# A hybrid encoder layer on one core: VectorE and ScalarE in written order within the attention stage

## The chip, the cores and the metric

The kernel runs on one core of a Trainium2 chip. A core has TensorE (matmuls, PE in the rows; PEld are its weight loads), VectorE (DVE), ScalarE (ACT), GpSimd (POOL) and SyncE (SP, which issues most DMAs). The metric is the time of one execution on the device in microseconds; lower is better. The kernel before takes 2234.18 us, the median of three runs (2233.41 to 2234.49).

## The reference

One layer of an encoder for 2048 tokens of width 1024: a modulated RMS norm, one input projection, windowed attention (8 query heads and 2 key heads of 64) beside a bidirectional mLSTM (4 heads of 128), a norm for each, one output projection, and a SwiGLU network. The attention and the place of the mLSTM's output gate `o_m` are what the change touches:

```python
proj = hmix @ w_in
q_a, k_a, v_a, q_m, k_m, v_m, o_m, gates = jnp.split(proj, IN_SPLITS, axis=-1)
att = banded_attention(q_a, k_a, v_a, sink)      # |t-s| <= 128, blocks of 128
att = rms_norm(att, g_attn_out)
...
h_m = rms_norm(h_fwd + h_bwd, g_mlstm_out)
h_m = jax.nn.sigmoid(o_m) * h_m
mix = jnp.concatenate([att, h_m], axis=-1) @ w_out
x = x + gate1 * mix

def banded_attention(q, k, v, sink):
    logits = q @ k.T * hd ** -0.5 - slope * dist     # three key blocks of 128
    mx = jnp.maximum(jnp.max(logits), sink)
    p = jnp.exp(logits - mx)
    p = p / (jnp.sum(p) + jnp.exp(sink - mx))
    return p @ v
```

## The kernel before

A float32 product is made of two or three matmuls on reduced-precision halves: a high half (ScalarE copies and rounds) and a low half (VectorE or GpSimd subtracts).

**The attention stage** is one loop over 32 units and two more steps (`for s_ in range(len(order) + 2)`). A unit is a block of 128 queries for one key head, that is four query heads. Three units are in work at a time. Of the newest, `u0`, each step makes the scores of four heads (`score`: two matmuls into `as` on L928 and L929, VectorE's maximum L932, ScalarE's exponential L934), then the reciprocal of the sum (`adn`) and, on GpSimd, the normalized scores `ap` (L948). Of the one before, `u1`, it makes three transposes (`transpose`: four TensorE instructions into `atp`, L955), each split by `split` into a high half `apth` (ScalarE) and a low half `aptl` (VectorE), both recorded on L140 and L141. Of the oldest, `u2`, it makes the product with the values (`values`: two matmuls for each of three blocks into `ao`, L967 with the high half, L968 with the low), which ScalarE and VectorE bring to `at`.

**Between these**, `pull(n)` puts in n matmuls of a projection that is due (`proj_mm`, tile `gps`, L640, three for each of eight slices of the weights: two with the high half `whi`, one with the low half `wlo`). What is due stands in `fill`: first the query columns of the last two attention heads (`second`, 96 matmuls), then the output-gate columns `o_tiles` of head 1 (96), then those of heads 2 and 3 together, in four parts (`lasts`, 48 each). `pull` also counts the beats after which a delayed action of `put_soon` is issued.

**The weights of a projection** come by `cols_steps`: SP loads 512 KB into `wraw`, a tile with one buffer; ScalarE makes `whi` (L235, 128x1024), GpSimd makes `wlo` in four pieces (L238, 128x256 each). `proj_cols` runs all of it at once. `o_tiles` calls `proj_cols` for all its heads when its first matmul is asked for, so in the program's text the conversions stand where that matmul stands.

**Order.** TensorE's order is the written one in the whole stage (a manual schedule). For VectorE, ScalarE, GpSimd and SP a scheduler orders the instructions; it may issue one ahead of where it is written. `finish_wo`, behind the loop, splits the output weights `wo` (four pairs of tiles of 128x1024); `first_pair` prepares the first tiles of the output projection between steps, and `Pair` holds the two pairs of token tiles with their squares (`msq`), sums (`aps`) and gates.

## Time and profile before

| what | value |
|---|---|
| median of three runs | 2234.18 us (2233.41 to 2234.49) |
| profiled execution | 2234.74 us, its span 2232.6 us |
| TensorE busy | 2211.5 us, 99% of the span |
| TensorE weight loads | 1864.0 us, 83% |
| VectorE | 1586.1 us, 71% |
| ScalarE | 1063.0 us, 48% |
| GpSimd | 1026.6 us, 46% |
| chain that ended last | 92% of it TensorE |

TensorE's matmuls are pipelined, and their ends are modelled: one starts every 0.23 us or so, though each is shown with 0.39. A wait of TensorE is therefore read from the distance of two starts, or from the idle time that a row names, and whether a wait of another engine costs time is read from whether TensorE has work meanwhile.

### The profile page before, as it was taken

What the parts mean: (1) busy time and instruction counts of PE and PEld (TensorE: products, weight loads), DVE (VectorE), ACT (ScalarE), POOL (GpSimd) and SP (SyncE); (2) the same over time, 40 slices, a digit from 0 to 9 for tenths busy, and PEclk for the clock granted to TensorE, in tenths of its full rate; (3) what the DMA queues carried; (4) which work ended last, traced back from release to release, by engine and by line L of the source; (5) the groups of instructions that cost most, each with busy time, mean ns of one, the idle gap of its engine ahead of it and who ended that gap; (6) DMA issues with size and microseconds to landing.
All of it is one profiled execution on the core that took longest, in us unless ns stands there. A gap on an engine that the chain in (4) does not pass through costs nothing.

```text
span 2232.6 us, 32512 instructions
## 1 busy us (share of the span) xinstructions
PE 2211.5 (99%) x10912; PEld 1864.0 (83%) x10912; DVE 1586.1 (71%) x2923; ACT 1063.0 (48%) x2215; POOL 1026.6 (46%) x901
## 2 busy tenths in 40 slices
PE   8999999999999999999999999999999999999998
PEld 8998888888888888888888888888888888888886
DVE  6866768656788898877766777776666665665794
ACT  6524665543778765354544435433433333333452
POOL 0018434444344344446666664566665663591020
PEclk9999999999999999999999999999999999999999
DMA  9468655776766667763353546334233374334552
GB/s 350 159 218 256 203 159 163 213 221 174 213 200 196 200 223 249 256 204 128 105 175 109 177 159 207 123 128 136 91 114 99 113 261 135 129 120 152 196 203 92
DMA packets 337063, 391.28 MB, mean 175 GB/s; under 512 B 20874, under 2 KB 234234, under 8 KB 336896
## 3 DMA queue, kind: packets, MB, share of 16 engines
q1 hardware_dynamic: 335216, 388.39, 53.7%
q8 instruction: 86, 1.41, 0.3%
q10 hardware_dynamic: 1680, 0.82, 0.1%
q14 instruction: 81, 0.66, 0.1%
HBM read 269.95 MB, written 119.19 MB: 174 GB/s over the span
## 4 chain that ended last, share of the span: by engine, by line
PE 92%; ACT 3%; DVE 3%; DMA 1%; issue 1%; SPq 0%; POOL 0%; ACTq 0%; DVEq 0%; POOLq 0%
PE gps L640 15%; PE fp L56 13%; PE fp L58 13%; PE fp L57 13%; PE fo L57 6%; PE fo L56 6%; PE fo L58 6%; PE ops L56 2%; PE ops L58 2%; PE ops L57 2%; PE num L856 1%; PE kvp L769 1%; ACT ap L934 1%; PE num L858 1%; PE pv L56 1%; PE pv L57 1%
## 5 line engine op out<-in xcount | busy, mean ns | idle before, releaser
L640 PE MATMUL gps<-hT,whi 128*128 128x512 f32 x1088 | 396.2, 418 | 0.0
L57 PE MATMUL fo<-w,ah 128*128 128x512 f32 x616 | 239.9, 390 | 0.0
L56 PE MATMUL fo<-w,ah 128*128 128x512 f32 x616 | 239.9, 389 | 0.0
L58 PE MATMUL fo<-w,al 128*128 128x512 f32 x616 | 239.8, 389 | 0.0
L640 PE MATMUL gps<-hT,wlo 128*128 128x512 f32 x544 | 226.5, 416 | 0.0
L640 PEld LDWEIGHTS gps<-hT,whi 128*128 128x128 f32 x1088 | 199.6, 189 | 23.6
L56 PE MATMUL fp<-T,S 128*128 128x512 f32 x528 | 206.5, 391 | 0.0
L58 PE MATMUL fp<-T,S 128*128 128x512 f32 x528 | 205.6, 389 | 0.0
L57 PE MATMUL fp<-T,S 128*128 128x512 f32 x528 | 205.5, 389 | 0.0
L1924 DVE TENSOR_TENSOR al<-al,ah 128x1024 fp32r<-128x1024 f32 x77 | 112.0, 1458 | 114.6 <-ACT ah L1923 114.4
L1923 ACT ACTIVATE ah<-al 128x1024 fp32r<-128x1024 f32 x77 | 81.6, 1060 | 173.5 <-DMA al<-a_d 172.1
L1622 DVE TENSOR_TENSOR S<-sf,S 128x512 fp32r<-128x512 f32 x86 | 122.7, 1463 | 37.4 <-ACT S L1621 37.2
L1622 DVE TENSOR_TENSOR A<-graw,A 128x512 fp32r<-128x512 f32 x86 | 124.9, 1473 | 17.4 <-ACT A L1621 17.3
L58 PE MATMUL fp<-B,A 128*128 128x512 f32 x352 | 137.0, 389 | 0.0
L56 PE MATMUL fp<-B,A 128*128 128x512 f32 x352 | 137.0, 389 | 0.0
L57 PE MATMUL fp<-B,A 128*128 128x512 f32 x352 | 137.0, 389 | 0.0
L56 PEld LDWEIGHTS fo<-w,ah 128*128 128x128 f32 x616 | 115.7, 188 | 24.3
L58 PEld LDWEIGHTS fo<-w,al 128*128 128x128 f32 x616 | 115.7, 188 | 24.2
L57 PEld LDWEIGHTS fo<-w,ah 128*128 128x128 f32 x616 | 115.7, 188 | 23.9
L948 POOL TENSOR_SCALAR ap<-ap,adn 128x384 f32<-128x384 f32 (+1 forms) x124 | 70.1, 584 | 128.4 <-PE atp L955 58.2
L1626 POOL TENSOR_TENSOR sf<-A,A22r 128x512 f32<-128x512 f32 x42 | 57.1, 1359 | 153.3 <-DMA A22r<-in_w_ffn_in_dram 142.4
L1791 DVE SCALAR_TENSOR_TENSOR g<-t,g 128x512 f32<-128x512 f32 x44 | 41.3, 938 | 120.5 <-ACT t L1790 120.5
(451 smaller groups left out, 6136.2 us busy)
## 6 DMA issues: line engine op xcount, KB each, us to landing
al<-a_d SPq DMA_DIRECT2D x77, 512.0 KB, 3.5
wmod<-in_w_mod_dram SPq DMA_DIRECT2D x48, 512.0 KB, 5.9
graw<-in_w_ffn_in_dram SPq DMA_DIRECT2D x43, 512.0 KB, 4.0
a_d<-ka SPq DMA_DIRECT2D x66, 256.0 KB, 4.7
bc<-bc_d SPq DMA_DIRECT2D x64, 256.0 KB, 4.6
hop_d<-n SPq DMA_DIRECT2D x56, 256.0 KB, 3.4
a_d<-u SPq DMA_DIRECT2D x55, 256.0 KB, 4.8
mqk<-qk_d SPq DMA_DIRECT2D x44, 256.0 KB, 4.5
```

Of the source, the lines that this page charges most:

```text
L56: pe.matmul(o, lh, rh, start=first, stop=False, skip_group_check=skip)
L57: pe.matmul(o, lh, rl, start=False, stop=False, skip_group_check=skip)
L58: pe.matmul(o, ll, rh, start=False, stop=last, skip_group_check=skip)
L640: pe.matmul(ps, w[i == 2][:, k, :], hT[n](i == 1, k), start=(k == 0 and i == 0), stop=(k == KT - 1 and i == 2))
L769: pe.matmul(kvp[:, :129], kn, vw, start=True, stop=True)
L856: pe.matmul(num[:, d, :129], sc[:, d, :], va_c, start=True, stop=st is None)
L948: pool.tensor_scalar(p, p, dn[:, g:g + 1], 0.0, MUL, ADD)
L1622: dve.tensor_tensor(t[:, 1, :], f, t[:, 0, :].bitcast(F32), SUB)
L1626: add.tensor_tensor(f1, a21, a22, ADD)
L1791: dve.scalar_tensor_tensor(g0, t0, 1.0, g0, ADD, MUL)
L1923: act.activation(ah, al.bitcast(F32), AF.Copy)
L1924: dve.tensor_tensor(al, al.bitcast(F32), ah.bitcast(F32), SUB)
```

## The change

Within the attention stage VectorE and ScalarE too are put into written order (a second manual schedule, `told`, over the loop and what stands behind it). The text is rearranged for it. `normalize` is cut in two, the exponential and sum (`rest_sum`) ahead of `leave`, which is the end of `values`. The low half of a unit's third transpose is issued behind the next unit's first maximum (`put_after(0)`). The splits of `wo` go into the loop, one pair per step, and the rest behind it. `nx2.gate()` moves ahead to the end of the stage. The DMA that ScalarE issues for `og_d` is delayed by four beats. `pull` puts three more projection matmuls ahead of the first unit's transposes and two more ahead of the last unit's; the number of matmuls in all is the same.

```diff
@@ o_tiles
-                (act if heads == (0,) and n > 0 else sp).dma_start(og_d[n, :, :, h], t.rearrange("p (c t) -> p c t", c=4))
+                o, v = og_d[n, :, :, h], t.rearrange("p (c t) -> p c t", c=4)
+                if heads == (0,) and n > 0:
+                    put_soon(4, act.dma_start, o, v)
+                else:
+                    sp.dma_start(o, v)
...
+    afters = ([], [])
+    def put_after(g, f):
+        afters[g].append(f)
+    def run_after(g):
+        while afters[g]:
+            afters[g].pop(0)()
@@ Unit.transpose
-            split(tp, hi, lo)
+            act.activation(hi, tp, AF.Copy)
             self.pt.append((hi, lo))
+            low = lambda: dve.tensor_tensor(lo, tp, hi.bitcast(F32), SUB)
+            if i == 2:
+                put_after(0, low)
+            else:
+                low()
@@ the loop
     u1 = u2 = None
+    told = ExitStack()
+    told.enter_context(tc.manual_schedule(engines={mybir.EngineType.DVE, mybir.EngineType.Activation}))
+    halves, since = deque(), 0
...
             if u0:
                 u0.score(g)
+            if g < 2:
+                run_after(g)
             pull(1)
...
         if u0:
-            u0.normalize(s_ in (0, len(order) - 1))
-        pull(1)
+            u0.rest_sum()
+        if u2:
+            u2.leave()
+        if u0 and s_ + 1 < len(order):
+            u0.normalize(s_ == 0)
+        pull({1: 4, len(order): 3}.get(s_, 1))
         for i in range(3):
             if u1:
                 u1.transpose(i)
+            if i == 1 and u0 and s_ + 1 == len(order):
+                u0.normalize(True)
             pull(1 if i == 0 or i == 2 and s_ % 2 else 2)
         u2, u1 = u1, u0
+        if halves and s_ > since + 1:
+            hi, lo = halves.popleft()
+            act.activation(hi, lo.bitcast(F32), AF.Copy)
+            put_after(1, lambda hi=hi, lo=lo: dve.tensor_tensor(lo, lo.bitcast(F32), hi.bitcast(F32), SUB))
...
-    finish_wo(0)
-    finish_wo(1)
+    for g in range(2):
+        run_after(g)
+    nx2.gate()
+    for hi, lo in halves:
+        act.activation(hi, lo.bitcast(F32), AF.Copy)
+        dve.tensor_tensor(lo, lo.bitcast(F32), hi.bitcast(F32), SUB)
+    told.close()
```

Two places show what moves. **Place A** is the unit in which the projection goes from the last query columns (`qhl` is its last output) to the output-gate columns of head 1. ScalarE's order before:

```order
L934 ACTIVATE ap,ars<-ap,nmx 128x384
L940 ACTIVATE adn<-adn 128x4
L140 ACTIVATE apth<-atp 128x512 x3
L692 ACTIVATE qhl<-gps 128x512
L235 ACTIVATE whi<-wraw 128x1024
L934 ACTIVATE ap,ars<-ap,nmx 128x384 x3
```

The conversion in it is that of a later head. ScalarE's order at the same place after the change, where the conversion is that of head 1:

```order
L948 ACTIVATE ap,ars<-ap,nmx 128x384
L954 ACTIVATE adn<-adn 128x4
L975 ACTIVATE apth<-atp 128x512
L692 ACTIVATE qhl<-gps 128x512
L235 ACTIVATE whi<-wraw 128x1024
L975 ACTIVATE apth<-atp 128x512 x2
L948 ACTIVATE ap,ars<-ap,nmx 128x384 x3
```

`qhl` and `whi` now stand between the first and the second `apth` of the unit; TensorE's next projection matmul, behind the first transposes, reads that `whi`.

**Place B** is the unit in which the projection goes from head 1 (`oth` is its last output) to heads 2 and 3. ScalarE's order before:

```order
L940 ACTIVATE adn<-adn 128x4
L140 ACTIVATE apth<-atp 128x512 x3
L717 ACTIVATE oth<-gps 128x512
L235 ACTIVATE whi<-wraw 128x1024
L1293 ACTIVATE ms_9114<-ma 128x256
L934 ACTIVATE ap,ars<-ap,nmx 128x384 x3
```

And after:

```order
L954 ACTIVATE adn<-adn 128x4
L975 ACTIVATE apth<-atp 128x512 x2
L717 ACTIVATE oth<-gps 128x512
L235 ACTIVATE whi<-wraw 128x1024 x2
L975 ACTIVATE apth<-atp 128x512
L948 ACTIVATE ap,ars<-ap,nmx 128x384 x3
```

Both conversions, for heads 2 and 3, now stand one behind the other and ahead of the unit's third `apth`. GpSimd's order at place B, with the numbers of the buffers, before:

```order
L948 TENSOR_SCALAR ap_9139<-ap_9139,adn_9162 128x384
L948 TENSOR_SCALAR ap_9152<-ap_9152,adn_9162 128x384
L238 TENSOR_TENSOR wlo_9218<-wraw_9215,whi_9217 128x256 x4
L948 TENSOR_SCALAR ap_9231<-ap_9231,adn_9273 128x384
L948 TENSOR_SCALAR ap_9241<-ap_9241,adn_9273 128x384
```

And after:

```order
L965 TENSOR_SCALAR ap_9144<-ap_9144,adn_9165 128x384
L965 TENSOR_SCALAR ap_9155<-ap_9155,adn_9165 128x384
L238 TENSOR_TENSOR wlo_9202<-wraw_9199,whi_9201 128x256 x4
L238 TENSOR_TENSOR wlo_9211<-wraw_9208,whi_9210 128x256 x4
L965 TENSOR_SCALAR ap_9235<-ap_9235,adn_9276 128x384
L965 TENSOR_SCALAR ap_9246<-ap_9246,adn_9276 128x384
```

Four low pieces have become eight, of two raw tiles that share the one buffer of `wraw`.

## Rows read from the trace of the kernel before

**Rows 1.** Windows: stretch, length, busy us PE PEld DVE ACT POOL, PEclk, DMA share, GB/s
```profile
560.00:800.00 240.00, 238.24 (x1289) 200.94 (x1288) 200.84 (x538) 183.46 (x467) 97.91 (x151) 1.00 0.69 209
...
2226.00:2228.00 2.00, 0.00 (x0) 0.00 (x0) 1.40 (x8) 0.32 (x2) 0.00 (x0) 1.00 0.14 55
2228.00:2230.00 2.00, 0.00 (x0) 0.00 (x0) 0.91 (x2) 0.72 (x1) 0.00 (x0) 0.62 0.09 35
```

**Rows 2.** Waits from 560 to 800 us: who, on whom; us, times, longest us
```profile
PEld ao L968 <- DVE aptl L141: 6.0, 16, 0.6
...
PEld atp L955 <- POOL ap L948: 1.4, 2, 0.9
```

**Rows 3.** Timeline of PE, first unit's transposes: start, us, instruction, [idle before]
```profile
569.42 1.19 PE L955 MATMUL atp<-ident,ap 128*128 128x128 f32 x4 [0.45 <-POOL ap L948]
```

**Rows 4.** Timeline of PE, last unit's transposes
```profile
764.28 0.44 PE L955 MATMUL atp<-ident,ap 128*128 128x128 f32 x2 [0.29 <-POOL ap L948]
```

**Rows 5.** The tile wraw, 560 to 720 us: ns min/median/max, first and last start
```profile
L235 ACT ACTIVATE whi<-wraw x3: 1043/1081/1082, 579.9 to 704.7; 128x1024 fp32r<-128x1024 f32 x3
...
DMA to landing us min/median/max: 5.2/5.2/5.2
```

**Rows 6.** Timeline of POOL behind the stage
```profile
771.00 0.45 POOL L1231 TENSOR_TENSOR msq<-msq 128x128 f32<-128x128 f32 x1
```

**Rows 7.** Timeline of PE behind the stage
```profile
771.34 0.58 PE L1279 MATMUL aps<-ones_r,msq 128*128 128x1 f32 x4
```

**Rows 8.** Timeline of ACT at place A
```profile
640.86 1.58 ACT L140 ACTIVATE apth<-atp 128x512 fp32r<-128x512 f32 x3
642.30 0.62 ACT L692 ACTIVATE qhl<-gps 128x512 fp32r<-128x512 f32 x1
642.78 1.08 ACT L235 ACTIVATE whi<-wraw 128x1024 fp32r<-128x1024 f32 x1
```

**Rows 9.** Timeline of PE at place A
```profile
639.50 0.48 PE L640 MATMUL gps<-hT,whi 128*128 128x512 f32 x1
...
640.49 0.39 PE L640 MATMUL gps<-hT,wlo 128*128 128x512 f32 x1
```

**Rows 10.** Timeline of POOL at place A
```profile
641.43 2.27 POOL L948 TENSOR_SCALAR ap<-ap,adn 128x384 f32<-128x384 f32 x4 [4.06 <-PE atp L955]
643.94 2.83 POOL L238 TENSOR_TENSOR wlo<-wraw,whi 128x256 fp32r<-128x256 f32 x4 [0.24 <-ACT whi L235]
```

**Rows 11.** Timeline of ACT at place B
```profile
702.75 1.58 ACT L140 ACTIVATE apth<-atp 128x512 fp32r<-128x512 f32 x3
```

**Rows 12.** Timeline of PE at place B
```profile
702.06 0.71 PE L640 MATMUL gps<-hT,whi 128*128 128x512 f32 x2
...
702.97 0.48 PE L640 MATMUL gps<-hT,wlo 128*128 128x512 f32 x1
...
706.17 0.39 PE L967 MATMUL ao<-apth,av 128*128 128x512 f32 x1
```

**Rows 13.** Timeline of POOL at place B
```profile
703.32 2.27 POOL L948 TENSOR_SCALAR ap<-ap,adn 128x384 f32<-128x384 f32 x4 [4.06 <-PE atp L955]
```

**Rows 14.** Timeline of SP behind place A
```profile
646.80 0.38 SPq L231 DMA_DIRECT2D wraw<-in_w_in_dram  x1
```

**Rows 15.** Timeline of DVE at place B
```profile
703.38 1.89 DVE L141 TENSOR_TENSOR aptl<-atp,apth 128x512 fp32r<-128x512 f32 x3 [0.24 <-ACT apth L140]
```

**Rows 16.** Timeline of PE at the kernel's start
```profile
9.05 2.50 PE L456 MATMUL warm<-xt,ident 128*128 128x128 f32 x10 [2.15 <-DMA xt<-in_x_dram]
11.35 4.61 PE L214 MATMUL modps<-scb,wmod 128*128 128x96 f32 x32
...
17.97 3.07 PE L214 MATMUL modps<-scb,wmod 128*128 128x96 f32 x24
...
21.94 1.98 PE L456 MATMUL warm<-ones_r,ident 128*128 128x128 f32 x16
```

## The prediction

> **What bounds the kernel now.** I read the windows first. Attention runs from 560 to 800 us, and in it TensorE is busy for 238.24 of 240.00 us at a granted clock of 1.00 [rows 1]. TensorE is the bound, its order is written by hand, and the change takes no matmul away and adds none. So there are two ways in which the time can move: by waits of TensorE that vanish (at most the 1.76 us of idle time, and what its weight loads wait beside it), or by new waits in front of its matmuls. The second view, the waits of the weight loads, tells what can vanish: 6.0 us in 16 waits on the low halves `aptl` of VectorE, and 1.4 us in two waits on the normalized scores `ap` of GpSimd [rows 2]. The third view is the timeline of each engine at the two units in which a projection changes its weight columns, since there the order of ScalarE moves most; those rows are cited below.

> **What the change takes away.** (1) The first unit's transposes wait for GpSimd's normalized scores: 0.45 us idle ahead of four transposes that then took 1.19 us [rows 3]. With three more projection matmuls ahead of them and the normalization issued without a wait for other work, this goes. At the last unit the same wait is 0.29 us [rows 4]. The two together are the 1.4 us of [rows 2]: −1.4. (2) The third low half used to stand ahead of the next unit's maxima, and the values' second matmul waited for low halves. Of the 6.0 us of weight-load waits [rows 2] only what exceeds the matmul running above them delays TensorE. The idle time of the stretch, 1.76 us [rows 1], less the 0.45 and 0.29 us just counted, leaves about 1.0; I take −1.0, between 0 (the waits stay, because the first two low halves are where they were) and −2.0. (3) The halves of the output weights are now split one per step instead of in a bunch: no TensorE wait stands on them in attention, and VectorE and ScalarE have room, so 0. Behind the last unit, though, one ScalarE copy of 128x1024 stays ahead of the squares `msq`; I price it like `whi`, the same shape, 1.08 us [rows 5]. GpSimd's sum of those squares ends at 771.45 and TensorE asks for it at 771.34 [rows 6, 7]: there is no slack, so +1.0 (0 to +1.5).

> **What it adds at place A**, where the projection's columns of head 1 begin. The order shows it: the conversion `whi` for the new columns was issued long ahead by the scheduler (the three conversions of before stand at 579.9, at 642.78 and at 704.67, a head early each [rows 5, 8]). In written order it is issued where the first matmul that needs it is written, directly behind the first transposes of a unit. ScalarE: `apth` begins at 640.86 and three of them last until the next start at 642.30, 0.48 each; `qhl` takes 0.48 to the next start, `whi` 1.08 [rows 8]. Now it is one `apth`, `qhl`, `whi`: 640.86 + 0.48 + 0.48 + 1.08 = 642.90. TensorE wanted the weights at 639.50 [rows 9]: 3.4 us of standing still. It then reaches the matmul with the low half 0.99 us later (639.50 to 640.49 [rows 9]), at 643.89. The low half is GpSimd's, which first normalizes, 641.43 + 2.27 = 643.70, and needs 2.83 / 4 = 0.71 for the first of four pieces [rows 10]: 644.41, 0.5 us late. A = 3.9. The lower bound is 2.5: if ScalarE stood free as soon as the transposes end, the three operations alone still take 2.04 us, and GpSimd's pieces come behind. The upper one is 5, if ScalarE comes 1 us later in its new order. Queued behind `whi` on ScalarE are the other two `apth`, which TensorE's own delay covers.

> **What it adds at place B**, where the columns of heads 2 and 3 begin together. ScalarE now has two `apth`, `oth`, both conversions, and only then the third `apth`. First conversion: 702.75 + 2 x 0.48 + 0.48 (`oth`, the shape and start-to-start time of `qhl`) + 1.08 = 705.27 [rows 8, 11]. TensorE wants it at 702.06 [rows 12]: 3.2 us. GpSimd's first low piece is ready at 703.32 + 2.27 + 0.71 = 706.30 [rows 10, 13]; TensorE wants it 0.91 us after its restart (702.06 to 702.97 [rows 12]), at 706.18: 0.1 us.
> The second conversion has its raw weights in the one buffer `wraw`, which is free only when the first conversion and all four low pieces have been made: 703.32 + 2.27 + 2.83 = 708.42. In before the pieces end at 643.94 + 2.83 = 646.77 and SP issues the next load at 646.80 [rows 10, 14], so SP waits for just that, and issues here at 708.45. The load lands 5.2 us after its issue [rows 5]: 713.65. Conversion: 714.73. Third `apth`: 715.21. TensorE, from its restart at 706.30 on, needs 706.17 − 702.97 = 3.20 us [rows 12] to the value matmul that reads the third `apth`: 709.50. It stands for another 5.7 us. The low half behind it costs VectorE 1.89 / 3 = 0.63 [rows 15], where the matmul that reads it is due some 0.2 later: 0.45; and VectorE's two maxima that were held up behind that low half push the first low half of the next unit, for which I take 0.3 (0 to 0.63). B = 3.2 + 0.1 + 5.7 + 0.45 + 0.3 = 9.8, with 7 below (ScalarE 1 us earlier at either stand, and nothing for VectorE) and 12 above (a load that is 2 us longer). SP stands from 705 to 708.5 behind that wait; what is queued there are loads for units two steps ahead, about 13 us away, and a store: 0.

> **The clock.** [...] I take it once: +1.8.
> [...]

> **Sum.** 3.9 + 9.8 + 1.8 − 1.4 − 1.0 + 1.0 = +14.1. The profiled execution took 2234.74 us, which gives 2248.8; against the median of 2234.18 it is 2248.3. I forecast 2248.3.

> **Rivals.**
> (a) The clock doesn't fall at B: 12.3 more than before, 2246.5. For it: at B TensorE works 3.2 us between its two stands. [...]
> (b) The clock falls at A as well: 2250.1. [...]
> (c) The second load at B takes twice its 5.2 us, since it falls into the attention loads that SP issues right behind it, and the DMA engines are 0.69 busy in the stretch [rows 1]: 2253.5. Against it: both loads of before landed in 5.2 in the same stretch.
> (d) The raw weights of head 3 are there in time (the edit doesn't couple the two conversions as I read it): B falls to 3.3 without a ramp, 3.9 + 3.3 − 1.4 = +5.8, 2240.0. Against it: the order has the two conversions next to each other, and one buffer.
> (e) Not slower: written order repairs all that attention loses. Its price is bounded by the idle time and the weight-load waits, 1.76 + 6.0 + 1.4 = 9.2 us [rows 1, 2]; with A and B at their lower bounds, 9.5, and the tail's 1.0 this gives +1.3, 2235.5. It decides from the point at which A and B together are under about 13 us and every weight-load wait was a delay of TensorE. Against it: most of these waits lie under running matmuls, or the idle time of TensorE would not be 1.76.

> **How the numbers follow.** Forecast 0.46, (a) 0.27, (b) 0.12, (c) 0.06, (d) 0.05, (e) 0.04. The range reaches from A and B at their lower ends without a ramp, 9.5 − 2.4 = +7.1 (2241), to (c) at 2254; outside lie (d), (e) and some of (c), about 0.13. About 0.2% (4.5 us) is what a measurement of this kernel can tell from no change: faster 0.01, same 0.04 (most of (e)), slower 0.95.

> **What would show it.** In the profile of after: at 640 to 643 TensorE idle ahead of `gps` on ScalarE's `whi`, 3 to 4 us; some 60 us later the same, and then a longer stand at `ao` on ScalarE's `apth`, with ScalarE itself idle ahead of `whi` until a DMA into `wraw`, and a granted clock below 1.00 there; no wait of the first unit's transposes on `ap`; weight-load waits on `aptl` well under 6.0; and the `aps` matmuls behind attention waiting for `msq`. The stretches outside 560 to 800 us keep their lengths. Wrong it would be if `whi` starts ahead of the `apth` that I put before it, if the second conversion at B finds its weights landed, or if the two stands show and the time is the same, so that attention regained what I hold to be covered.

## The result, and the profile after

The changed kernel takes 2258.14 us (four runs, 2256.38 to 2259.75) against 2234.03 before: 24.1 us more, a ratio of 1.0106 with a 95% interval of 1.0094 to 1.0118. The forecast was slower, by 14.1 us; the sign was right and 10 us were missing. The profiled execution after is the longest of the four (2259.75); its span is 2257.9 us, 25.3 more than the 2232.6 before.

To see where they went, the two traces are laid on each other at TensorE's own landmarks, whose order the change leaves alone: the first scores matmul of each step, the matmuls `aps` that sum squares behind the stage, and `arb`, which spreads the root. The table says by how much the changed kernel's distance between two landmarks exceeds that of before, in us.

| stretch | after − before | forecast for it |
|---|---|---|
| up to step 2 (first unit's transposes) | −1.6 | −1.1 |
| steps 2 to 12 | +0.9 | share of −1.0 |
| steps 12 and 13 (place A) | +5.8 | +3.9 |
| steps 14 to 22 | −0.1 | share of −1.0 |
| steps 22 and 23 (place B) | +9.6 | +9.8, and 1.8 for the clock |
| steps 24 to 31 | +3.1 | share of −1.0 |
| step 31 to `aps` | +3.3 | −0.3 |
| `aps` to `arb` | +4.6 | +1.0 |
| behind it | −0.3 | 0 |

(The forecast's −1.4 for the two waits is divided here as 1.1 for the first unit and 0.3 for the last. Of the −1.6, 1.05 lie ahead of the stage, where nothing was changed; in the stage it is −0.5, with three more matmuls of 0.23 in it, so a gain of 1.2. Step 31 to `aps` has two more, 0.5 us. Behind `arb` the five are missing, 1.15 us of work, and yet only 0.3 are gained there.) A, B and the clock together came to 15.4 where 15.5 were forecast. All that is missing lies in the rows that the forecast held to be nearly free.

**Place A**, in the timeline of TensorE of the kernel after; [rows 9] are the same matmuls before:

```profile
638.65 0.60 PE L972 MATMUL atp<-ident,ap 128*128 128x128 f32 x4
642.39 0.50 PE L640 MATMUL gps<-hT,whi 128*128 128x512 f32 x1 [3.15 <-ACT whi L235]
...
643.91 0.60 PE L640 MATMUL gps<-hT,wlo 128*128 128x512 f32 x1 [0.34 <-POOL wlo L238]
```

ScalarE's order there is the one read from the program, `apth`, `qhl`, `whi` (in [rows 8] the conversion stood behind all three `apth`):

```profile
640.31 0.60 ACT L975 ACTIVATE apth<-atp 128x512 fp32r<-128x512 f32 x1
640.81 0.59 ACT L692 ACTIVATE qhl<-gps 128x512 fp32r<-128x512 f32 x1
641.28 1.06 ACT L235 ACTIVATE whi<-wraw 128x1024 fp32r<-128x1024 f32 x1
```

TensorE stands for 3.15 us and, for the low half, 0.34 more: forecast 3.4 and 0.5.

**Place B**, TensorE after (before: [rows 12]):

```profile
710.19 0.73 PE L640 MATMUL gps<-hT,whi 128*128 128x512 f32 x2 [2.95 <-ACT whi L235]
...
718.62 0.50 PE L989 MATMUL ao<-apth,av 128*128 128x512 f32 x1 [4.01 <-ACT apth L975]
719.35 0.79 PE L990 MATMUL ao<-aptl,av 128*128 128x512 f32 x1 [0.22 <-DVE aptl L977]
```

and ScalarE:

```profile
709.07 1.07 ACT L235 ACTIVATE whi<-wraw 128x1024 fp32r<-128x1024 f32 x1
717.03 1.06 ACT L235 ACTIVATE whi<-wraw 128x1024 fp32r<-128x1024 f32 x1 [6.89 <-DMA wraw<-in_w_in_dram]
717.99 0.58 ACT L975 ACTIVATE apth<-atp 128x512 fp32r<-128x512 f32 x1
```

The second conversion waits 6.89 us for the load into the one buffer, and the third `apth` and TensorE with it, as forecast. The load was issued when the low pieces were done and was there after 3.8 us, not the 5.2 of [rows 5], so the second stand is 4.0 and not 5.7:

```profile
713.26 0.38 SPq L231 DMA_DIRECT2D wraw<-in_w_in_dram  x1
```

**The clock**, in windows of the kernel after (stretch, length, busy us of PE, PEld, DVE, ACT, POOL, granted clock, DMA share, GB/s):

```profile
642.00:644.00 2.00, 1.26 (x7) 0.89 (x7) 0.00 (x0) 0.91 (x2) 2.00 (x5) 1.00 0.98 296
644.00:648.00 4.00, 4.00 (x14) 3.44 (x15) 1.69 (x4) 0.96 (x3) 1.92 (x3) 0.57 0.28 76
...
714.00:718.00 4.00, 0.61 (x4) 0.23 (x2) 0.00 (x0) 0.97 (x2) 0.00 (x0) 1.00 0.48 131
718.00:722.00 4.00, 3.16 (x9) 2.45 (x10) 2.74 (x9) 3.28 (x10) 2.79 (x4) 0.66 0.11 33
...
795.00:800.00 5.00, 5.00 (x13) 3.98 (x14) 2.70 (x16) 0.60 (x1) 0.00 (x0) 0.50 1.05 383
```

In windows of half a microsecond it is 1.00 up to 719.0, 0.76 in the next, 0.50 in each from 719.5 to 722.5, and 0.83 in the next; so the values between are read as means over a stretch that has both 1.00 and 0.50. It fell three times, not once: after A (0.57 from 644 to 648), after the second stand at B (0.66 from 718 to 722; from 714 to 718, in the stand, it still was 1.00), and behind the stage (0.50 from 795 to 800).

**The end of the stage.** The sums of squares, which ended at 771.45 in [rows 6], now come 1.1 us too late for TensorE, and again 0.83 us:

```profile
793.54 0.38 PE L1304 MATMUL aps<-ones_r,msq 128*128 128x1 f32 x2 [1.10 <-POOL msq L1256]
794.76 0.59 PE L1304 MATMUL aps<-ones_r,msq 128*128 128x1 f32 x2 [0.83 <-POOL msq L1256]
```

GpSimd made them beside two operations of VectorE, the last split of the output weights and the gate, which the change had moved there (first two rows GpSimd, last two VectorE):

```profile
790.85 1.25 POOL L1255 TENSOR_TENSOR msq<-msq 128x256 f32<-128x256 f32 x1 [8.17 <-ACT msq L1254]
792.17 1.32 POOL L1256 TENSOR_TENSOR msq<-msq 128x128 f32<-128x128 f32 x1
```

```profile
790.28 1.22 DVE L1377 TENSOR_TENSOR wo<-wo 128x1024 fp32r<-128x1024 f32 x1 [0.16 <-ACT wo L1376]
791.42 1.76 DVE L1274 SCALAR_TENSOR_TENSOR mm<-og,mm 128x1024 f32<-128x1024 f32 x1
```

The second of them is a sum of 128x128, which took 0.45 in [rows 6]; the first took 0.74 before:

```profile
768.95 0.74 POOL L1230 TENSOR_TENSOR msq<-msq 128x256 f32<-128x256 f32 x1 [4.73 <-ACT msq L1229]
```

Then TensorE ran at a granted clock of 0.50 up to the root (795 to 800, above). Ahead of all this, TensorE's longest wait between step 31 and `aps` is for the third `apth` of the last unit:

```profile
783.09 0.50 PE L989 MATMUL ao<-apth,av 128*128 128x512 f32 x1 [0.94 <-ACT apth L975]
```

**The steps in between.** The waits of the stage after, 560 to 820 us (who, on whom; us, times, longest):

```profile
PEld ao L990 <- DVE aptl L977: 11.9, 25, 1.2
...
PE ao L990 <- DVE aptl L977: 3.7, 13, 0.8
```

The 6.0 us in 16 waits of [rows 2] have become 11.9 in 25. The reason can be read in one step of VectorE:

```profile
741.75 0.61 DVE L946 CUSTOM_DVE_ANT_0 ap<-as,abias,nsk 128x384 f32<-128x384 f32 x1
...
743.82 0.68 DVE L997 TENSOR_TENSOR at<-ao,at 64x512 f32<-64x512 f32 x1 [0.66 <-ACT at L993]
...
745.14 1.29 DVE L977 TENSOR_TENSOR aptl<-atp,apth 128x512 fp32r<-128x512 f32 x2 [0.25 <-ACT apth L975]
746.41 0.52 DVE L1320 TENSOR_TENSOR ms<-ms 128x128 f32<-128x128 f32 x1
746.97 0.56 DVE L1322 TENSOR_TENSOR ms<-ms 128x128 f32<-128x128 f32 x1
747.45 0.60 DVE L946 CUSTOM_DVE_ANT_0 ap<-as,abias,nsk 128x384 f32<-128x384 f32 x1
...
747.99 0.68 DVE L977 TENSOR_TENSOR aptl<-atp,apth 128x512 fp32r<-128x512 f32 x1
...
749.12 0.61 DVE L946 CUSTOM_DVE_ANT_0 ap<-as,abias,nsk 128x384 f32<-128x384 f32 x1
```

and of ScalarE:

```profile
743.20 0.59 ACT L993 ACTIVATE at<-ao 64x512 f32<-64x512 f32 x1
...
744.51 1.58 ACT L975 ACTIVATE apth<-atp 128x512 fp32r<-128x512 f32 x3
...
748.10 0.61 ACT L948 ACTIVATE ap<-ap,nmx 128x384 f32<-128x384 f32 x1 [1.72 <-DVE nmx L946]
```

Start at the third maximum, 741.75. ScalarE's third exponential follows it, then `at`; VectorE's half of `at` waits for that (0.66), and the low halves wait for `apth` (0.25). Behind the low halves stand two sums `ms` for the first output pair, and behind them the next unit's first maximum, the held-back low half, and two more maxima; the third is at 749.12. Meanwhile ScalarE waits 1.72 us for the first maximum. In written order that is a closed loop through both engines: once round takes 749.12 − 741.75 = 7.37 us here, where most of TensorE's steps before the change took 6.2 to 6.6 (the two steps that it falls into took 6.97 and 6.18 before, and 7.50 and 7.14 after). TensorE pays at the end of the loop, at the value matmul that reads the held-back low half:

```profile
748.72 0.50 PE L990 MATMUL ao<-aptl,av 128*128 128x512 f32 x1 [0.49 <-DVE aptl L977]
```

That is the reading. The runs below test it.

### The profile page after: what moved, and what is told of

It reads as the page before. It is cut to its first block, busy times and chain, and to the rows that moved or that the text cites. A ratio compares the mean times of both kernels' runs of the same rounds, so it can differ in the third digit from the quotient of the medians.

```text
span 2257.9 us, 32515 instructions
## 1 busy us (share of the span) xinstructions
PE 2221.7 (98%) x10912; PEld 1868.4 (83%) x10912; DVE 1588.8 (70%) x2923; ACT 1066.7 (47%) x2215; POOL 1028.7 (46%) x901
## 4 chain that ended last, share of the span: by engine, by line
PE 64%; DVE 0%; POOL 0%; ACT 0%; issue 0%; ACTq 0%
PE fp L56 12%; PE fp L58 12%; PE fp L57 12%; PE fo L57 6%; PE fo L58 6%; PE fo L56 6%; PE ops L56 2%; PE ops L58 2%; PE ops L57 2%; PE gps L640 1%; PE trn L1523 0%; PE trn L185 0%; PE arb L1267 0%; PE aps L1304 0%; POOL msq L1255 0%
## 5 line engine op out<-in xcount | busy, mean ns | idle before, releaser
L58 PEld LDWEIGHTS fo<-w,al 128*128 128x128 f32 x616 | 115.6, 188 | 24.1
```

Of the source, the lines that this page charges most:

```text
L58: pe.matmul(o, ll, rh, start=False, stop=last, skip_group_check=skip)
```

## The experiments

Two theories stood against each other. **Theory 1:** late weights at A and B, three edits at the stage's end, and a closed loop of VectorE and ScalarE in written order are separate causes, and together all of the loss. **Its rivals:** TensorE would be held at A and B by other late work anyway; VectorE's sum of work, not its order, is too much; or written order costs something in every step. For each run the table gives the same stretches as above (growth against the kernel before, us, from one profiled execution each) and the median with the 95% interval of its ratio.

| run | 2–12 | A | 14–22 | B | 24–31 | 31–`aps` | –`arb` | behind | median us | ratio |
|---|---|---|---|---|---|---|---|---|---|---|
| after | 0.9 | 5.8 | −0.1 | 9.6 | 3.1 | 3.3 | 4.6 | −0.3 | 2258.14 | 1.0094–1.0118 |
| e1 weights early | 1.0 | 0.2 | 0.5 | −0.1 | 4.8 | 3.3 | 3.1 | −1.5 | 2244.53 | 1.0034–1.0059 |
| e2 end of stage back | 0.9 | 5.3 | 0.1 | 10.7 | 3.1 | 1.8 | 0.0 | 1.2 | 2255.88 | 1.0081–1.0108 |
| e3 VectorE alone in order | 1.7 | 0.3 | 0.0 | 0.0 | 4.3 | 0.3 | 2.2 | −0.7 | 2241.35 | 1.0020–1.0043 |
| e4 ScalarE alone in order | 1.8 | 4.6 | −0.6 | 10.9 | 1.5 | 1.6 | 2.5 | −0.7 | 2253.32 | 1.0069–1.0096 |
| e6 = e1 + e2 | 1.0 | 0.2 | 0.4 | 0.0 | 4.8 | 1.8 | 0.0 | 1.1 | 2243.01 | 1.0028–1.0054 |
| e7 = e6, no pair on VectorE | 1.2 | 0.2 | 0.5 | 0.0 | −0.7 | 1.4 | 0.0 | 3.2 | 2238.19 | 1.0010–1.0028 |
| e8 = e6 + dose ahead of the maxima | 15.1 | 2.0 | 0.8 | −0.1 | 4.8 | 1.8 | 0.0 | 1.2 | 2258.91 | 1.0099–1.0130 |
| e9 = before + same dose | 5.2 | 0.6 | 0.0 | 0.0 | 0.0 | 0.0 | 0.0 | 0.0 | 2239.65 | 1.0016–1.0036 |
| e13 = e6 + dose in the wait | 3.3 | 0.2 | 0.5 | −0.1 | 4.9 | 1.8 | 0.0 | 1.3 | 2245.66 | 1.0038–1.0066 |
| e10 = e7 mended | 1.0 | 0.2 | 0.5 | 0.0 | 3.8 | 0.6 | 0.5 | 0.0 | 2239.51 | 1.0016–1.0034 |
| e11 = e10, third low half back | 1.8 | 0.4 | 1.3 | 0.0 | 3.1 | 2.1 | 0.4 | 0.6 | 2242.95 | 1.0024–1.0050 |
| e14 = e10, gate in the wait | 1.0 | 0.2 | 0.5 | −0.1 | −0.7 | 1.4 | 0.4 | 0.1 | 2236.12 | 0.9999–1.0018 |
| e5 = before + pulls | 0.4 | −0.1 | 1.3 | 1.1 | 1.1 | 0.0 | 0.0 | 0.0 | 2236.32 | 1.0003–1.0020 |

(In all but e9, 31–`aps` holds 0.5 us for the two matmuls moved there, and “behind”, from `arb` to the end, has five fewer, 1.15 us.)

### Late weights: e1, e3, e4

e1 issues the loads and conversions of the three heads ahead of their use, from the loop:

```diff
+    early = [cols_steps(C_OM + h * P) for h in (1, 2, 3)]
...
+        if s_ in (2, 13, 21):
+            next(early[(2, 13, 21).index(s_)])
+        if s_ in (4, 16, 23):
+            u = (4, 16, 23).index(s_)
+            *_, cols_ = early[u]
+            (wo1, wo23, wo23)[u].append(cols_)
```

> The changed kernel, with the weights of heads 1, 2 and 3 loaded and converted a unit or more before their first matmul (conversions at the end of the steps 4, 16 and 23 of the attention loop); all else as changed. In the changed kernel's trace the steps with place A add 5.8 us over before and those with place B 9.6. Theory (the stands at A and B are caused by conversions issued too late, and are local): both vanish, 2258.1 - 15.4 = 2242.7 us. Rival 1 (ScalarE has no room in written order, each earlier conversion costs its own 1.1 us): 2246. Rival 2 (TensorE would be held at those places by other late work anyway): over 2252.

13.6 us came back, and the stretches of A and B are at 0.2 and −0.1: the stands were caused by the late conversions alone, and nothing else was behind them. Steps 24 to 31 grew by 1.7 us against the kernel after, 1.4 of it in step 24, right behind B (−0.2 there in the kernel after, +1.2 in e1). A likely reading, not tested by itself, is that the long stand at B had given VectorE and ScalarE time to catch up.

e3 and e4 put only one of the two engines into written order:

```diff
-    told.enter_context(tc.manual_schedule(engines={mybir.EngineType.DVE, mybir.EngineType.Activation}))
+    told.enter_context(tc.manual_schedule(engines={mybir.EngineType.DVE}))
```

> The changed kernel with only VectorE in written order; ScalarE is ordered by the scheduler again, which issues the conversions of heads 1 and 2 long ahead. Theory 1 (A and B belong to ScalarE's order, the rest of the loss to VectorE's): 2258.1 - 15.4 = 2242.7 us. Theory 2 (the rest needs both engines in written order, since each then waits for the other within a step): 2237 or less. Rival (A and B stay, because GpSimd's low halves or the load set them): 2255.

> The changed kernel with only ScalarE in written order; VectorE is ordered by the scheduler again. A and B stay in every theory. Theory 1 (the rest of the loss belongs to VectorE's order): 2234.0 + 15.4 = 2249.4 us or a little less. Theory 2 (the rest needs both): the same 2249.4, and then the run with VectorE alone is at 2237. Rival (the rest belongs to ScalarE's order too): 2258.

e3 has no stand at A or B, e4 has both: they belong to ScalarE's order. For the rest the answer is not the clean one of either theory. With VectorE alone, steps 24 to 31 still lose 4.3 us, so its order suffices for that part; but with ScalarE alone the steps 2 to 12 and 24 to 31 lose 3.3 and the end 4.1, so ScalarE's order has a share too. e4 at 2253.3 lies between theory 1 and the rival.

### The end of the stage: e2 and e6

```diff
-            if i == 1 and u0 and s_ + 1 == len(order):
+            if i == 2 and u0 and s_ + 1 == len(order):
                 u0.normalize(True)
...
-        if halves and s_ > since + 1:
+        if halves and since + 1 < s_ <= len(order):
...
-    nx2.gate()
-    for hi, lo in halves:
-        act.activation(hi, lo.bitcast(F32), AF.Copy)
-        dve.tensor_tensor(lo, lo.bitcast(F32), hi.bitcast(F32), SUB)
...
         nx2.square(i, sq[:, i])
+    for hi, lo in halves:
+        act.activation(hi, lo.bitcast(F32), AF.Copy)
...
     nxt.s4()
+    nx2.gate()
```

and the low part of that split behind the diagonals.

> The changed kernel, with the end of the stage as before in three points: the gate of the second pair back behind the sums, the last split of the output weights behind the squares, and the last unit's normalization behind the third high half instead of ahead of it. The changed kernel loses 4.5 us from the last unit's scores to the sums of squares and 3.4 us more to the matmuls that spread the root. Theory (these three edits stand in the way there): about 5 us of the 7.9 come back, 2253. Rival (VectorE and ScalarE arrive late at the end because of the 30 units before, and the three edits only stand in the queue): 1 us, 2257.

> The edits of the two runs before (weights early, end of the stage as before) together. Sum rule: the early weights gave 13.6 us, the end 2.3 (median) to 4.9 (profile, from the last unit's maxima to the root). Theory (the places are independent): 2244.5 - 2.3 to 4.9, that is 2239.6 to 2242.2 us, and the drift of 4.8 us between the steps 24 and 31 stays. Rival (the drift grows when A and B no longer hold TensorE back, and takes the gain): 2244.

The wait of `aps` is gone in both, 4.6 us of the kernel after. GpSimd's sums take in e2 what they took before:

```profile
789.58 0.74 POOL L1255 TENSOR_TENSOR msq<-msq 128x256 f32<-128x256 f32 x1 [5.76 <-ACT msq L1254]
790.39 0.46 POOL L1256 TENSOR_TENSOR msq<-msq 128x128 f32<-128x128 f32 x1
```

The stretch ahead of it, where the normalization was moved, fell from 3.3 to 1.8. But the medians fell by only 2.3 (e2) and 1.5 (e6 against e1): part is given back behind the stage, where TensorE in e6 now waits for VectorE's sums `xr`, which in VectorE's order stand behind the moved split and gate, among others.

```profile
803.00 0.49 PE L56 MATMUL ops<-wo,mS 128*128 128x512 f32 x1 [0.92 <-DVE xr L1433]
809.73 0.47 PE L56 MATMUL ops<-wo,mS 128*128 128x512 f32 x1 [0.98 <-DVE xr L1433]
```

### The closed loop: e7, and two doses

e7 takes the first pair's sums and its gate out of the loop:

```diff
-                dve.tensor_tensor(t[:, 2 + i], f, g, ADD)
+                pool.tensor_tensor(t[:, 2 + i], f, g, ADD)
...
-        cur.gate()
...
     nx2.diagonal(r[:, 2:4], diag())
+    nxt.gate()
```

> As the run above, and in addition VectorE is freed of the work of the first output pair within the steps 21 to 29: its sums of squares go to GpSimd and its gate (1.52 us in the changed kernel) behind the stage. Theory (in written order VectorE and ScalarE form a closed loop within a step, about as long as TensorE's step, so that each extra operation in it delays TensorE): the drift between steps 24 and 31 falls from 4.8 us to under 1.5, and the time is 3 to 4 us below the run above, 2237. Rival (the drift comes from the last maximum and low half being moved, whatever else VectorE does): no change against the run above.

The growth of 4.8 us in the steps 24 to 31 is gone (−0.7). In e6's trace 3.7 of the 4.8 lie in the steps 24 to 27, in which VectorE makes the sums, and 0.8 in step 30, in which it makes the gate. e8 and e9 put the same twenty VectorE additions, which change nothing that is read, into ten quiet steps, and e13 puts twenty at another place of the step:

```diff
+        if 2 <= s_ < 12:
+            for _ in range(2):
+                dve.tensor_tensor(u1.p[3][:, :u1.NK], u1.p[3][:, :u1.NK], u1.p[3][:, :u1.NK], ADD)
         u2, u1 = u1, u0
```

> As the run with weights and end mended, with two extra VectorE additions of 128x384 over dead scores at the end of each of the steps 2 to 11, where nothing else is added. Theory of the closed loop: the ten steps grow by most of what is added, 0.9 us each less at most 0.3 of room: +6 to +9 us. Rival (VectorE has room, being busy 0.8 of the stretch): under +1.5.

> The kernel before with the same twenty additions written at the same place; the scheduler sets where VectorE issues them. Theory of the closed loop (it is the written order that closes it, a free order fills waits): under +2.5 us. Rival (VectorE's load itself is the limit in attention, in either order): as much as in written order, +6 to +9.

e13's edit stands behind `rest_sum`, ahead of `leave`:

```diff
             u0.rest_sum()
+        if 2 <= s_ < 12:
+            for _ in range(2):
+                dve.tensor_tensor(u2.pt[0][1][:, :384], u2.pt[0][1][:, :384].bitcast(F32), u2.pt[0][1][:, :384].bitcast(F32), ADD)
         if u2:
             u2.leave()
```

> The run with weights and end mended, with two extra VectorE additions of 128x384 in each of the steps 2 to 11, as in the dose run, but behind the fourth maximum, where VectorE waits 0.7 us for ScalarE in each step. Theory (it is the loop of waits that sets the step, so an operation in a wait is partly free): the ten steps grow by 1.6 - 0.7 us each, +7 to +10 where the first dose gave +16. Rival (VectorE's sum of work sets the step): +16 again.

The twenty additions in the groups of lines of VectorE, 570 to 660 us, of e8, e9 and e13 (busy us, mean ns):

```profile
L1376 DVE TENSOR_TENSOR ap<-ap 128x384 f32<-128x384 f32 x20 | 15.8, 792 | 0.3
```

```profile
L1339 DVE TENSOR_TENSOR ap<-ap 128x384 f32<-128x384 f32 x20 | 12.6, 630 | 0.0
```

```profile
L1365 DVE TENSOR_TENSOR aptl<-aptl 128x384 fp32r<-128x384 f32 x20 | 11.7, 586 | 0.3
```

Ahead of the maxima 15.8 us of additions cost 15.9 (2258.91 − 2243.01), all of it. In the wait 11.7 us cost 2.65, less than the 7 to 10 expected, which had counted 1.6 us a step where these took 1.17. (In e8 they were longer, 0.79 us each against 0.59; why was not shown.) In the free order of the kernel before 12.6 us cost 5.8, more than the bound of 2.5 and just under the rival's 6. So VectorE's sum of work is not what sets the step; where in the chain an operation stands is. From 570 to 645 us VectorE waits for ScalarE's `at` and `apth` 3.4 and 3.7 us in e6, 6.2 and 3.0 in e8, and 0.3 and 0.4 in e13. VectorE in e8, with the dose in the chain and the wait still there:

```profile
593.38 1.71 DVE L1376 TENSOR_TENSOR ap<-ap 128x384 f32<-128x384 f32 x2
...
598.81 0.68 DVE L997 TENSOR_TENSOR at<-ao,at 64x512 f32<-64x512 f32 x1 [0.78 <-ACT at L993]
```

and in e13, with the dose in place of the wait (here 1.76 us, in the other nine steps 1.14 or 1.15):

```profile
595.39 1.76 DVE L1365 TENSOR_TENSOR aptl<-aptl 128x384 fp32r<-128x384 f32 x2
597.07 0.68 DVE L997 TENSOR_TENSOR at<-ao,at 64x512 f32<-64x512 f32 x1
```

### Does written order cost anything by itself? e10, e14, e11

e7 still lost 4.3 us behind the stage (it ends 3.2 later there with 1.15 less work), most of it in waits for `xr`. e6 loses 2.2 there in the same waits; what e7 loses beyond that is read as its gate, which stands ahead of `xr` on VectorE, and no run has it alone. e10 moves that gate to GpSimd within the stage and splits two `wo` pairs in one late step:

```diff
-    nxt.gate()
...
+        def gate_pool(self):
+            pool.tensor_tensor(self.og, self.og, self.m, MUL)
+            pool.tensor_tensor(self.m, self.m, self.og, ADD)
...
+        cur.gate_pool()
...
+        for _ in range(2 if s_ == len(order) else 1):
```

> The run without the pair's work on VectorE, with its own side effects mended: the first pair's gate on GpSimd within the stage, and the last split of the output weights one step earlier, both out of the output projection's way, where that run lost 4.3 us behind the stage. Theory (weights, end of stage and the closed loop are all there is): 2234 to 2235, as before the change. Rival (written order itself costs more in every step): 2238 as the run before.

The theory failed: 2239.5. Up to step 30 e10 was 0.3 us later than the kernel before, then it lost 4.2 us in one step. TensorE waits 0.46 us for `apth` and 1.88 for `aptl` there, and behind these waits, from 753.43 to 756.10, a matmul of 128x512 starts 0.42 or 0.43 us ahead of the next and one of 128x384 0.32, where from 752.47 to 753.05 it is 0.23 and 0.17 or 0.18. VectorE and GpSimd in that step:

```profile
746.82 2.03 DVE L953 TENSOR_TENSOR adn<-nmx,skb 128x4 f32<-128x4 f32 x1
...
749.38 1.92 DVE L958 TENSOR_TENSOR adn<-adn,ars 128x4 f32<-128x4 f32 x1
```

```profile
746.45 2.39 POOL L1275 TENSOR_TENSOR og<-og,mm 128x1024 f32<-128x1024 f32 x1 [2.09 <-DMA og<-og_d]
748.92 2.36 POOL L1276 TENSOR_TENSOR mm<-mm,og 128x1024 f32<-128x1024 f32 x1
```

Two additions of 128x4, which take 0.16 each in the next step, end when GpSimd's operations end (746.82 + 2.03 = 748.85 against 746.45 + 2.39 = 748.84, and 751.30 against 751.28). e14 has the gate on VectorE, in the wait that e13 had found:

```diff
+        if s_ + 2 == len(order):
+            nxt.gate()
+            nx2.load_gate()
         if u2:
             u2.leave()
```

> The run with the loop mended, but the first pair's gate neither on GpSimd nor ahead of the maxima: on VectorE behind the fourth maximum of the step before the last unit's transposes, where the second dose of 1.6 us cost only 0.2 us a step. In the run with the loop mended two VectorE operations on 128x4 took 2.03 and 1.92 us beside the two GpSimd operations of that gate, TensorE lost 4.2 us in that step, and the stage was 0.3 us behind the kernel before until then. Theory (written order costs nothing in itself once weights, end of stage and closed loop are mended): 2234 to 2236 us. Rival (the 4.2 us belong to the last steps of the written order, whichever engine makes the gate): 2239.

2236.12, which is 2.2 us more than before, a ratio of 0.9999 to 1.0018: with the weights early, the end mended and nothing extra in the loop, written order costs between nothing and 4 us. Its stretches still hold 1.0 in the steps 2 to 12, 0.5 in 14 to 22 and 0.9 ahead of `aps` (beside the two matmuls), which no run explains. Written order also brings nothing; no version was faster than the kernel before.

e11 puts the third low half back ahead of the first maximum in e10:

> The run with the loop mended, and the third low half issued where it was, ahead of the next unit's first maximum. Theory (in the closed loop only the sum of VectorE's work counts, and ScalarE waits over 1 us ahead of its first exponential): within 1.5 us of the run with the loop mended, the waits of the values' second matmul on low halves rather fewer. Rival (the delayed low half is what lets the maxima come in time): 4 to 8 us slower.

3.4 us slower by the medians, so neither the theory's 1.5 nor the rival's 4 to 8; but the intervals of e10 and e11 overlap (1.0016 to 1.0034, 1.0024 to 1.0050). That holding the low half back helps in written order is likely from this, and not shown beyond doubt.

### The moved projections: e5

```diff
-        pull(1)
+        pull({1: 4, len(order): 3}.get(s_, 1))
```

> The kernel before with only one part of the change: three more projection matmuls ahead of the first unit's transposes and two more ahead of the last unit's. Theory (the two waits for the normalized scores, 1.4 us of weight-load waits, go, and nothing else is late): 2232.6 us. Rival (the transposes wait for other work at the same time): 2234.

2.5 us slower. The gain at the first unit is there (TensorE has 0.7 us more work there and is not later), and so is that ahead of `aps` (0.5 us more work, and not later). But none of it reaches the end: behind `arb` five matmuls are missing, 1.15 us, and that stretch is as long as before, with TensorE now waiting for the first `mS` tiles, 0.41 us for one of them. And 3.5 us are lost in the steps 14 to 31. The scheduler has set a new order for ScalarE, though only TensorE's text was changed: around 692 us a square for the first pair now stands ahead of an `apth` and waits for its load, where before it stood behind all three (first fence e5, second the kernel before). That step, 21, grew by 1.1 us; the other 2.4 were not traced to a cause.

```profile
692.25 0.42 ACT L1293 ACTIVATE ms<-ma 128x256 f32<-128x256 f32 x1 [2.11 <-DMA ma<-mxa_d]
692.57 0.58 ACT L140 ACTIVATE apth<-atp 128x512 fp32r<-128x512 f32 x1
```

```profile
690.09 1.57 ACT L140 ACTIVATE apth<-atp 128x512 fp32r<-128x512 f32 x3
691.61 0.42 ACT L1293 ACTIVATE ms<-ma 128x256 f32<-128x256 f32 x1
```

## Why the prediction was wrong

**Right.** That two stands would appear, where, behind which operations, and by which chain at B (conversion, low pieces, SP, load, conversion, `apth`); e1 took both away. The first unit's gain: 1.2 against 1.1, though e5 shows that it does not reach the end of the kernel. The sum for A, B and the clock came to 15.4 where 15.5 were forecast, but that is luck: two errors met. The load at B landed after 3.8 us instead of 5.2. And the clock fell at A as well (rival (b)), 0.57 from 644 to 648: A cost 5.8, of which 3.5 are its two stands; the rest lies behind them. No run shows the 1.8 us that the sum has for the clock, the ramp, by itself. What the kernel after showed in its place, behind B's second stand, is a granted clock of 0.76 from 719.0 to 719.5, 0.50 from 719.5 to 722.5 and 0.83 from 722.5 to 723.0; an estimate from these windows (0.24 of 0.5 us, 0.50 of 3.0 and 0.17 of 0.5) is 1.7 us lost there.

**Wrong, the first step:** the attention steps. The prediction gives them −1.0 for the low halves, and of the work that written order puts elsewhere in a step it says only, of the output weights' halves, that "VectorE and ScalarE have room, so 0". No row is named for that room; the busy times of [rows 1], 200.84 and 183.46 of 240 us, would suggest it. The room is there, but in written order it lies at fixed places, waiting for the other engine. What is added elsewhere in the loop is paid in full (e8: 15.9 us for 15.8 us of work). The steps 2 to 12, 14 to 22 and 24 to 31 lost 3.9 us instead of winning 1.0. The splits of the output weights are not to blame, the first of them stands at 774 us, behind step 30. For 24 to 31 e7 names the operations, the output pair's sums and gate, which the prediction nowhere priced. For the 0.9 to 1.0 of the steps 2 to 12, where nothing was added, no run names the operation: they stay in e14.

**Wrong, the second step:** the end of the stage, −0.3 and +1.0 against +3.3 (of which 0.5 are the two matmuls moved there) and +4.6. Two edits were not priced there at all. The last unit's normalization, in written order ahead of the third `apth`, held that back, and TensorE waited 0.94 us for it; e2, which moves it, the last split and the gate, has 1.5 less in that stretch. And `nx2.gate()`, moved ahead, ran with the last split beside GpSimd's sums, which took 1.25 and 1.32 us in place of 0.74 and 0.46. GpSimd's four sums lasted from 790.85 to 794.70, 3.85 us, against 2.5 before (768.95 to 771.45); so by an estimate from these rows some 1.35 of the 1.9 us by which the `aps` were late are their length, and the rest is left for the late copy on ScalarE, the prediction's +1.0. From 794.0 to 794.5, in the second wait of the `aps`, the granted clock was 0.85, and 0.50 from 795 to 800. e2 moved gate and split together, so how the 4.6 us divide between them is open.

The kernel after and e10 both have operations of the two engines that were longer beside each other. In the kernel after, GpSimd's third and fourth sums, of the same two shapes, took 0.71 and 0.45 us from 793.46 on, where VectorE was idle. In e10 VectorE's addition of 128x4 took 2.03 us, to the end of GpSimd's operation, and 0.16 a step later. Neither run shows the cause.

The rest of the prediction's own tests: weight-load waits on `aptl` were to fall well under 6.0 and rose to 11.9, which alone contradicts the −1.0.

## What to carry to other kernels

When a scheduled engine is put into written order, look first for what the scheduler had issued early, weight conversions and loads above all: a conversion written where its first reader stands cost its whole chain here. Then follow one step's chain through all engines in their written order and compare its length with the bound engine's step; a busy share did not show the room in a closed loop here. Put extra work into the waits of that loop, not ahead of its first link: here that made the difference between 2.65 us and 15.9.
